# Moving the first B tiles of a fused matmul and RMS norm to the software DMA queue, and splitting A's first load over both hardware queues

## The chip, the cores and the metric

The kernel runs on one core of a Trainium2 chip. The metric is the device time of one execution in microseconds. TensorE is called PE below, VectorE DVE, ScalarE ACT, GpSimd POOL and SyncE SP. DMAs that SP and ACT issue run on the hardware queues, those of GpSimd on the software queue.

## The reference

```python
m, k, n = 2048, 2048, 2048            # a, b, gamma float32
x = np.matmul(a, b)
rms = np.sqrt(np.mean(x ** 2, axis=-1, keepdims=True) + eps)
return (gamma * x / rms).astype(np.float32)
```

## The kernel before

The first four blocks of 128 rows ("the head") are computed while A and B still arrive. The contraction goes by eight pairs of 128: a pair takes 512 rows by 256 columns of A (0.5 MB in fp32) and 256 rows of B's left half (1 MB in fp32, cast to bf16). A is transposed on PE. The first pair comes over the hardware queues in fp32 and is cast on the core; all later pairs come over the software queue, which casts in flight.

```python
    # first pair: hardware queues, fp32
    nc.sync.dma_start(out=a0f, in_=a[0:HB * P, 0:W2].rearrange("(r p) k -> p r k", p=P))
    for t in range(2):
        nc.scalar.dma_start(out=b0f[t], in_=b[t * P:(t + 1) * P, 0:HALF])
    ...
    def load_b(j, kp):                       # software queue, fp32 -> bf16
        nc.gpsimd.dma_start(
            out=raw[j][kp],
            in_=b[kp * W2:(kp + 1) * W2, j * HALF:(j + 1) * HALF].rearrange(
                "(t p) n -> p t n", p=P))

    def load_head(kp):                       # A block, then B tile, of one pair
        nc.gpsimd.dma_start(
            out=ah(kp),
            in_=a[0:HB * P, kp * W2:(kp + 1) * W2].rearrange("(r p) k -> p r k", p=P))
        load_b(0, kp)
    ...
    load_head(1)
    identity_f = t_left[:, 2, KP - 1, 0:2 * P].bitcast(FP32)
    make_identity(nc, identity_f)
    for kp in range(2, 4):
        load_head(kp)
    ...                                      # 11 warm-up matmuls on PE
    def transpose_first():
        ...                                  # 8 fp32 transposes into view[0], view[1]
        for t in range(2):
            cast_first = [lambda: nc.vector.tensor_copy(out=raw[0][0][:, t, :CH],
                                                        in_=b0f[t][:, :CH]),
                          lambda: nc.scalar.copy(out=raw[0][0][:, t, CH:], in_=b0f[t][:, CH:])]
            move = [lambda h=h: nc.vector.tensor_copy(
                out=head_at[:, t, 2 * h:2 * h + 2, :], in_=view[t][:, 2 * h:2 * h + 2, :])
                for h in range(2)]
            for work in (cast_first + move if t == 0 else move + cast_first):
                work()
    ...
    for kp in range(KP):                     # the head, left half
        if kp + 4 < KP:
            load_head(kp + 4)
        ...                                  # 14 matmuls, transposes of the next pair, 2 matmuls
```

In what follows, pairs are counted from one: "the second pair's B tile" is `raw[0][1]`, "the fifth" is `raw[0][4]`.

Of the kernel before, what the change touches and what calls it, by code (L numbers as in the profile page):

```python
# [8 lines left out]
FP32 = mybir.dt.float32  # L9
# [8 lines left out]
def kernel(  # L18
# [13 lines left out]
    nc = tc.nc  # L32
    P = 128
# [4 lines left out]
    W2 = 2 * P  # L38
    MB = M // P
    CH = 512  # L40
    NCH = N // CH
    HALF = N // 2
    HB = 4
# [15 lines left out]
    early = consts.tile([P, 6 * 2048], BF16, name="early")  # L59
    head_at = consts.tile([P, KT, HB, P], BF16, name="head_at")  # L60
    raw = [[consts.tile([P, 2, HALF], BF16, name=f"b_{j}_{kp}") for kp in range(KP)]
           for j in range(2)]
# [2 lines left out]
    sums = [t_left, t_right]  # L65

    a0f = early[:, 0:2048].bitcast(FP32).rearrange("p (r k) -> p r k", r=HB)
    b0f = [early[:, 2048 + t * 2048:2048 + (t + 1) * 2048].bitcast(FP32) for t in range(2)]
    NAH = 6
    ah_slot = [early[:, 6144 + s * 1024:6144 + (s + 1) * 1024].rearrange("p (r k) -> p r k", r=HB)  # L70
               for s in range(NAH)]
# [16 lines left out]
        return (at_even, at_odd)[(mb // 2) % 2][:, mb % 2]  # L88


    nc.sync.dma_start(out=a0f, in_=a[0:HB * P, 0:W2].rearrange("(r p) k -> p r k", p=P))
    for t in range(2):
        nc.scalar.dma_start(out=b0f[t], in_=b[t * P:(t + 1) * P, 0:HALF])

    def ah(kp):
        return ah_slot[(kp - 1) % NAH]

    def load_b(j, kp):
# [5 lines that stand above are left out]
    def load_head(kp):  # L104
# [4 lines that stand above are left out]
# [15 lines left out]
    def wait_for(src):  # L124

        nc.gpsimd.tensor_copy(out=pace, in_=src)

    load_head(1)
    identity_f = t_left[:, 2, KP - 1, 0:2 * P].bitcast(FP32)
    make_identity(nc, identity_f)  # L130
# [19 lines left out]
    def transpose_first():  # L150
        bank = [ps_t.tile([P, CH], FP32, name="tbank"), ps_a.tile([P, CH], FP32, name="acc")]
        view = [b.rearrange("p (r m) -> p r m", r=HB) for b in bank]
        for t in range(2):
            for r in range(HB):
                nc.tensor.matmul(view[t][:, r, :], a0f[:, r, t * P:(t + 1) * P], identity_f,
                                 is_transpose=True, start=(r == 0), stop=(r == HB - 1))
        for t in range(2):
            cast_first = [lambda: nc.vector.tensor_copy(out=raw[0][0][:, t, :CH],
                                                        in_=b0f[t][:, :CH]),
                          lambda: nc.scalar.copy(out=raw[0][0][:, t, CH:], in_=b0f[t][:, CH:])]  # L160
            move = [lambda h=h: nc.vector.tensor_copy(
                out=head_at[:, t, 2 * h:2 * h + 2, :], in_=view[t][:, 2 * h:2 * h + 2, :])
                for h in range(2)]
            for work in (cast_first + move if t == 0 else move + cast_first):
                work()

    def transpose_head(kp):
        bank = ps_t.tile([P, CH], FP32, name="tbank")
# [263 lines left out]
    for r in range(HB):  # L432
        x_tile(r, 0)
    early_sums = {4: ((2,), 0, 6), 5: ((5,), 0, 7), 6: ((1,), 0, KP)}
    transpose_first()
    for kp in range(KP):
        if kp + 4 < KP:
# [393 lines left out]
```

## Time and profile before

| | before |
|---|---|
| median of 3 runs | 222.53 us (222.32 to 222.62) |
| span of the profiled execution (a run of 222.97 us) | 221.2 us |
| PE busy | 95% of the span |
| A's first load landed, last engine | 6.26 us |
| B's first two tiles landed, last engine | 5.13 and 8.68 us |
| second pair's B tile landed, last engine | 12.26 us |
| fifth pair's B tile landed, last engine | 25.05 us |

The landings are read from the semaphore increments in the trace. A DMA here is complete when all sixteen engines have added theirs, so a tile is there when its slowest engine is.

First the chain of waits that ended last, in order of time: start, length, what. DMA pieces run from issue to landing.

```profile
5.65 0.70 POOL b L99
...
6.70 0.65 POOL early L105
7.35 17.70 DMA b<-in_b_dram
25.05 0.04 issue
25.10 1.67 PE acc L384 x7
26.77 0.45 PE tbank L172 x8
27.21 1.51 PE acc L384 x7
28.73 0.43 PE tbank L415 x2
29.16 1.51 PE acc L384 x7
...
68.17 139.98 PE acc L289 x648
```

From the fifth pair's B tile on, PE never waits until 208.2 us; before it the chain is that tile's DMA. A pair costs PE 1.51+0.45+1.51+0.43 = 3.9 us, and the software queue delivers one every 3.83 us (16.08 less 12.26, the last engine's landings of the second and the third pair's B tiles). The two are so close that PE cannot catch up: a tile that comes late anywhere in the head is paid in full.

The timeline of the first microseconds (start, busy time, engine, line, operation, and in brackets the idle time before it and who ended it):

```profile
0.74 0.46 SPq L91 DMA_DIRECT2D early<-in_a_dram  x1
0.74 0.90 ACTq L93 DMA_DIRECT2D early<-in_b_dram  x2
...
1.25 0.94 POOL L105 DMA_DIRECT2D early<-in_a_dram  x1 [0.80 <-POOLq L812]
...
7.54 2.88 PE L384 MATMUL acc<-b,head_at 128*128 128x512 bf16 x12
...
8.70 0.62 ACT L160 CAST b<-early 128x512 bf16<-128x512 f32 x1 [2.93 <-DMA early<-in_b_dram]
...
12.30 1.67 PE L384 MATMUL acc<-b,head_at 128*128 128x512 bf16 x7
...
25.10 1.67 PE L384 MATMUL acc<-b,head_at 128*128 128x512 bf16 x7 [0.85 <-DMA b<-in_b_dram]
```

PE's second pair starts at 12.30, as soon as its B tile is there (12.26), and before the fifth pair PE waits 0.85 us. Last, the table of windows: stretch, its length, busy time of PE, PEld (PE's weight loads), DVE, ACT and POOL with their counts, granted clock, mean DMA share, GB/s. The GB/s count bytes as written, so a load that casts reads twice as much.

```profile
4.00:6.00 2.00, 1.87 (x6) 0.55 (x4) 0.74 (x1) 0.62 (x1) 2.00 (x4) 1.00 1.06 350
6.00:8.00 2.00, 1.52 (x11) 1.08 (x12) 0.94 (x3) 0.00 (x0) 2.00 (x11) 1.00 0.80 214
8.00:10.00 2.00, 2.00 (x10) 0.86 (x9) 0.91 (x3) 0.62 (x1) 0.10 (x1) 1.00 1.31 207
```

The last line is the software stream: 207 GB/s written, 414 read. Up to 8 us almost all traffic is the hardware queues' (the DMA records show the first software packet at 6.27 us).

### The profile page before, as it was taken

How to read it: one execution, taken by the hardware profiler on the slowest of the kernel's cores; microseconds unless marked ns; L12 is line 12 of the kernel's file. 1: busy time of each engine (PE TensorE's matmuls, PEld its weight loads, DVE VectorE, ACT ScalarE, POOL GpSimd, SP SyncE). 2: the span in 40 equal slices, each digit the busy share in tenths (PEclk: the TensorE clock that was granted, in tenths of full speed). 3: DMA queues.
4: the chain of work that ended last, by engine and by line, in shares of the span. 5: the costliest groups of instructions: out<-in, count | busy, mean ns of one | idle time of the engine just before them, and what ended most of it. 6: DMA issues, size and time to landing. Idle time of an engine off the chain costs nothing.

```text
span 221.2 us, 3022 instructions
## 1 busy us (share of the span) xinstructions
PE 210.0 (95%) x1035; PEld 97.7 (44%) x1035; DVE 167.4 (76%) x330; ACT 128.1 (58%) x263; POOL 29.4 (13%) x59
## 2 busy tenths in 40 slices
PE   7899899999999999999999999999999999999950
PEld 2445454444455444444444444444444444444430
DVE  2428789999988898969696639855794759797691
ACT  3110001830698898678945997389738995334570
POOL 7634323220000001200110002000200000000040
PEclk9999999999999999999999999999999999999996
DMA  6999999999938596956799249955798349044045
GB/s 184 223 202 209 203 208 210 211 211 238 426 114 357 187 291 120 316 230 150 219 308 397 79 88 266 367 221 95 187 302 367 69 90 381 32 190 193 1 190 191
DMA packets 36321, 47.13 MB, mean 213 GB/s; under 512 B 21969, under 2 KB 26065, under 8 KB 34897
## 3 DMA queue, kind: packets, MB, share of 16 engines
q0 software_dynamic: 9936, 23.33, 41.7%
q1 hardware_dynamic: 25936, 22.29, 33.6%
q10 hardware_dynamic: 432, 1.31, 2.0%
q8 instruction: 8, 0.13, 0.2%
q14 instruction: 9, 0.07, 0.1%
HBM read 34.60 MB, written 16.78 MB: 232 GB/s over the span
## 4 chain that ended last, share of the span: by engine, by line
PE 83%; DMA 8%; POOL 3%; DVE 2%; issue 1%; ACT 1%; DVEq 0%; ACTq 0%; POOLq 0%
PE acc L289 69%; PE acc L384 12%; DMA b<-in_b_dram 8%; POOL early L105 1%; POOL b L99 1%; DVE x L709 1%; PE tbank L415 1%; PE tbank L172 1%; DVE x L712 1%; ACT sq L307 0%; PE tbank L189 0%; PE acc L189 0%; DVE a L709 0%; ACT sq L778 0%; DVE x L786 0%
## 5 line engine op out<-in xcount | busy, mean ns | idle before, releaser
L289 PE MATMUL acc<-b,s 128*128 128x512 bf16 x408 | 92.1, 379 | 0.0
L289 PEld LDWEIGHTS <-s 128*128 128x128 f16 (+1 forms) x512 | 49.9, 98 | 59.9 <-DVE s L264 0.4
L384 PE MATMUL acc<-b,head_at 128*128 128x512 bf16 x176 | 41.9, 379 | 1.0 <-DMA b<-in_b_dram 0.9
L307 ACT ACTIVATE sq<-x 128x512 bf16<-128x512 f32 x54 | 34.0, 630 | 6.9 <-DVE x L709 3.0
L366 DVE SCALAR_TENSOR_TENSOR x<-x,r,gamma_sb 128x1024 f32<-128x1024 f32 x28 | 34.8, 1281 | 0.7
L223 ACT ACTIVATE sq<-a 128x1024 bf16<-128x1024 f32 x24 | 25.3, 1054 | 2.4 <-DMA a<-in_a_dram 1.9
L384 PEld LDWEIGHTS <-head_at 128*128 128x128 bf16 x176 | 16.8, 98 | 20.6 <-issue 1.9
L246 ACT ACTIVATE head_at<-a,s 128x2048 f16<-128x2048 f32 x10 | 20.0, 1998 | 3.7 <-DVE s L233 3.7
L426 ACT COPY x<-acc 128x512 f32<-128x512 f32 x6 | 3.4, 586 | 25.7 <-PE acc L384 25.7
L289 PEld LDWEIGHTS <-head_at 128*128 128x128 f16 (+1 forms) x112 | 10.9, 98 | 13.2
L289 PE MATMUL acc<-early,head_at 128*128 128x512 bf16 x64 | 14.5, 379 | 0.0
L289 PEld LDWEIGHTS <-at_even 128*128 128x128 f16 x96 | 9.4, 98 | 11.3
L289 PE MATMUL acc<-early,s 128*128 128x512 bf16 x56 | 14.4, 379 | 0.0
L264 DVE TENSOR_TENSOR s<-head_at 128x1024 f16<-128x1024 f16 (+5 forms) x22 | 13.4, 635 | 0.1
L596 DVE TENSOR_TENSOR x<-x,x 128x512 f32<-128x512 f32 x9 | 6.2, 692 | 8.8 <-ACT x L594 8.3
L99 POOL DMA_DIRECT2D b<-in_b_dram x15 | 10.6, 706 | 16.0 <-DMA b<-in_b_dram 13.4
L578 ACT COPY x<-acc 128x512 f32<-128x512 f32 x9 | 5.2, 574 | 11.6 <-PE acc L289 11.5
L289 PE MATMUL acc<-t_left,s 128*128 128x512 bf16 x48 | 11.3, 379 | 0.0
L280 DVE TENSOR_TENSOR b<-b 128x1024 bf16<-128x1024 bf16 x16 | 10.8, 684 | 0.2
L289 PE MATMUL acc<-t_left,head_at 128*128 128x512 bf16 x48 | 10.9, 379 | 0.0
L289 PE MATMUL acc<-t_left,at_even 128*128 128x512 bf16 x48 | 10.8, 379 | 0.0
L289 PE MATMUL acc<-early,at_even 128*128 128x512 bf16 x48 | 10.8, 379 | 0.0
(111 smaller groups left out, 216.7 us busy)
## 6 DMA issues: line engine op xcount, KB each, us to landing
out_dram<-x SPq DMA_DIRECT2D x30, 512.0 KB, 3.8
a<-in_a_dram POOLq DMA_DIRECT2D x10, 1024.0 KB, 8.7
b<-in_b_dram POOLq DMA_DIRECT2D x15, 512.0 KB, 17.5
a<-in_a_dram POOLq DMA_DIRECT2D x4, 512.0 KB, 16.6
early<-in_a_dram POOLq DMA_DIRECT2D x7, 256.0 KB, 14.8
early<-in_b_dram ACTq DMA_DIRECT2D x2, 512.0 KB, 5.9
gamma_sb<-in_gamma_dram POOLq DMA_DIRECT2D x1, 1024.0 KB, 14.8
early<-in_a_dram SPq DMA_DIRECT2D x1, 512.0 KB, 5.5
```

The costliest lines, as they stand in the source:

```text
L99: nc.gpsimd.dma_start(out=raw[j][kp], in_=b[kp * W2:(kp + 1) * W2, j * HALF:(j + 1) * HALF].rearrange("(t p) n -> p t n", p=P))
L223: nc.scalar.activation(out=junk, in_=a32[mb][:, h * HALF:(h + 1) * HALF], func=ACTF.Square, scale=2.0 ** -8, accum_out=n2[:, h:h + 1])
L246: nc.scalar.activation(out=a16[mb], in_=a32.pop(mb), func=ACTF.Copy, scale=factor.pop(mb))
L264: nc.vector.tensor_tensor(out=sum_of(g, s)[:, lo:hi, :], in0=x[:, lo:hi, :], in1=y[:, lo:hi, :], op=op)
L280: nc.vector.tensor_tensor(out=flat[:, 1:3, :], in0=flat[:, 1:3, :], in1=flat[:, 0::3, :], op=ALU.add)
L289: nc.tensor.matmul(bank, lhsT[:, kp, :], rhs, start=(start and kp == 0), stop=(kp == KP - 1), skip_group_check=not start)
L307: nc.scalar.activation(out=sq[:, 0:CH], in_=src, func=ACTF.Square, scale=inv_sqrt_n, accum_out=msq[mb][:, c:c + 1])
L366: nc.vector.scalar_tensor_tensor(out=x, in0=x, scalar=inverse_of[mb], in1=gamma_sb[:, h * HALF:(h + 1) * HALF], op0=ALU.mult, op1=ALU.mult)
L384: nc.tensor.matmul(bank, head_at[:, kt, r, :], head_rhs(c, kt), start=(kt == 0), stop=(kt == KT - 1))
L426: copy(out=x_chunk(*g), in_=banks[g])
L578: nc.scalar.copy(out=c, in_=one[1])
L596: nc.vector.tensor_tensor(out=t, in0=t, in1=x12, op=ALU.add)
```

## The change

The intent: the stream of the software queue is the bottleneck of the head, and it seems to start late because 1.5 MB in fp32 go before it on slower hardware queues. So only A's 0.5 MB stay there, by halves on both queues; B's first tiles join the faster software stream, which casts them, and four casts on the core disappear. The copies of the transposes are shared by DVE and ACT.

```diff
-    nc.sync.dma_start(out=a0f, in_=a[0:HB * P, 0:W2].rearrange("(r p) k -> p r k", p=P))
-    for t in range(2):
-        nc.scalar.dma_start(out=b0f[t], in_=b[t * P:(t + 1) * P, 0:HALF])
+    for h, queue in enumerate((nc.sync, nc.scalar)):
+        queue.dma_start(out=a0f[:, 2 * h:2 * h + 2, :],
+                        in_=a[2 * h * P:(2 * h + 2) * P, 0:W2].rearrange("(r p) k -> p r k", p=P))
...
+    for t in range(2):
+        nc.gpsimd.dma_start(out=raw[0][0][:, t, :], in_=b[t * P:(t + 1) * P, 0:HALF])
     load_head(1)
...
-        for t in range(2):
-            cast_first = ...          # DVE and ACT cast B's tile t
-            move = ...                # DVE copies the transposes
-            for work in (cast_first + move if t == 0 else move + cast_first):
-                work()
+        for t, copy in enumerate((nc.vector.tensor_copy, nc.scalar.copy)):
+            for h in range(2):
+                copy(out=head_at[:, t, 2 * h:2 * h + 2, :], in_=view[t][:, 2 * h:2 * h + 2, :])
```

More of the change, by code (lines that the diff above doesn't have):

```diff
@@ L67 @@
     a0f = early[:, 0:2048].bitcast(FP32).rearrange("p (r k) -> p r k", r=HB)
-    b0f = [early[:, 2048 + t * 2048:2048 + (t + 1) * 2048].bitcast(FP32) for t in range(2)]
     NAH = 6
@@ L156, in transpose_first @@
                                  is_transpose=True, start=(r == 0), stop=(r == HB - 1))
-        for t in range(2):
-            cast_first = [lambda: nc.vector.tensor_copy(out=raw[0][0][:, t, :CH],
-                                                        in_=b0f[t][:, :CH]),
-                          lambda: nc.scalar.copy(out=raw[0][0][:, t, CH:], in_=b0f[t][:, CH:])]
-            move = [lambda h=h: nc.vector.tensor_copy(
-                out=head_at[:, t, 2 * h:2 * h + 2, :], in_=view[t][:, 2 * h:2 * h + 2, :])
-                for h in range(2)]
-            for work in (cast_first + move if t == 0 else move + cast_first):
-                work()
+        for t, copy in enumerate((nc.vector.tensor_copy, nc.scalar.copy)):
+            for h in range(2):
+                copy(out=head_at[:, t, 2 * h:2 * h + 2, :], in_=view[t][:, 2 * h:2 * h + 2, :])
     def transpose_head(kp):
```

## The prediction

> **What bounds the kernel now.** From 25.1 us to 208.2 us TensorE is the whole chain of waits, with no idle stretch. Before that the chain is one piece: 17.7 us of "DMA b<-in_b_dram" (7.35 to 25.05 us), the fifth B tile of the software queue. The timeline shows TensorE paced by B earlier too: the tiles of pairs 1 and 3 land at 12.26 and 20.14 us, their matmuls start at 12.30 and 20.18. A pair costs TensorE 3.9 us (1.51+0.45+1.51+0.43 in the chain) and the software queue 3.83 us (landing to landing). So everything after 25.05 us moves with the landing of the fifth B tile, and that moves with the moment the software stream starts at full rate.
>
> **What the first loads do now.** By the DMA records the hardware queues carry A's 0.5 MB and B's 1 MB from about 1.6 to 8.5 us, at about 230 GB/s. The software queue, issued at 1.25 us, has its first packet at 6.3 us, few until 8 us, and then reads about 420 GB/s (a 1 MB B tile, cast, per 2.48 us; a 0.5 MB A block per 1.3 us). Its first A block lands at 9.72 us, so it starts, in effect, at 8.45.
>
> **What changes.** The hardware queues keep only 0.5 MB. B's 1 MB goes ahead of the software stream, with the cast. Removed: four casts (0.62, 0.62, 0.74, 0.43 us) on VectorE and ScalarE. Two transposed halves (0.37 us each) move to ScalarE. GpSimd gets two more issues (0.5 to 0.7 us each) before the identity; the warm-up matmuls run to 5.9 us, so this has slack. The Trainium skill (DMA: Bandwidth & Descriptors, SWDGE vs HWDGE vs iDMA) says that a cast in flight needs the software path; the same page gives that path about 1 us to the first byte. The trace agrees where the queues are quiet: 1.25 us at 64.3 us.
>
> **Sum (estimate).** A's two halves land near 4.5 us. B needs 1 MB at 420 GB/s, 2.5 us, mostly behind them: first tile near 5.7, second near 7. The stream then starts in effect near 7.0 instead of 8.45: 1.4 us earlier: pair 1's B tile near 10.8, the fifth tile near 23.6. TensorE starts on the first pair near 7.1 (7.54 now), reaches pair 1 near 11.0 (12.30 now) and follows. I discount 0.2 us for a late software start. All of it is on the critical path.
>
> Predicted: 221.3 us, range 220.2 to 222.7. Faster by over 2%: 0.01; within 2%: 0.98; slower: 0.01.
>
> **What would show it.** Software queue's first packets at 2.5 to 4.5 us; A landing before 5.5; first pair's matmuls running without the gap around 9 us; pair 1's B tile landing near 10.8; the DMA piece of the chain ending near 23.6; the rest of the chain 183 us as now.
>
> **What would make it wrong.** (1) The 6.3 us is the software path's own cold start, not hardware traffic ahead of it: then B's second tile lands at 8.8 us and the stream starts 0.3 us later than now; gain zero or a small loss. (2) The fifth tile is late partly because one of the 16 engines lags: its last landings come 1.5 us after the others, following a 16 KB instruction fetch at 20 to 22 us. If that lag falls elsewhere, up to about 1 us more is won; or lost. (3) ScalarE's copies hold the first matmuls.

## The result

The changed kernel took 222.84 us (median of 4 runs, 222.49 to 223.03), the kernel before 222.57 us beside it: a ratio of 1.0012, 95% interval 0.9998 to 1.0027. Ratios are computed as the mean time of one kernel's runs over that of the other's of the same rounds, so they are not quite the ratio of the medians quoted. The predicted 1.2 us did not come, and the time lies just above the predicted range (220.2 to 222.7). Measured again on another chip it was 222.47 us beside 222.76, ratio 0.9992 (0.9974 to 1.0010).

| last engine's landing, us | before | before again | changed | changed again | predicted |
|---|---|---|---|---|---|
| A's first load | 6.26 | 6.37 | 4.27 | 4.23 | 4.5 |
| B's first two tiles | 5.13, 8.68 | 5.21, 8.76 | 6.92, 8.76 | 6.23, 8.68 | 5.7, 7 |
| second pair's B tile | 12.26 | 12.34 | 12.59 | 12.53 | 10.8 |
| the same, mean of 16 engines | 11.98 | 11.94 | 11.84 | 11.74 | |
| fifth pair's B tile | 25.05 | 24.63 | 24.54 | 24.48 | 23.6 |
| span of the profiled run | 221.2 | 221.1 | 220.7 | 220.7 | |

The spans look 0.4 us better, but the four profiled runs are not like the timed ones: the two of the kernel before took 222.97 and 222.87 us, slower than most of its runs, and those of the changed kernel 222.49 and 222.44, at its fast end. The timed runs decide: no gain.

The chain of waits of the changed kernel:

```profile
1.23 0.71 POOL b L128
1.95 6.81 DMA b<-in_b_dram
8.76 0.29 issue
9.05 15.50 DMA b<-in_b_dram
24.59 1.67 PE acc L379 x7
26.26 0.45 PE tbank L167 x8
26.70 1.51 PE acc L379 x7
28.21 0.43 PE tbank L410 x2
28.65 1.51 PE acc L379 x7
```

It now starts with B's first load itself, which takes 6.8 us from issue to landing. The chain still names the fifth pair's tile, but PE was all but ready for it: it waited 0.10 us there (0.85 in the kernel before). Its timeline, for the same places:

```profile
0.74 0.45 SPq L91 DMA_DIRECT2D early<-in_a_dram  x1
...
1.23 1.25 POOL L128 DMA_DIRECT2D b<-in_b_dram  x2 [0.79 <-POOLq L807]
...
7.42 2.76 PE L379 MATMUL acc<-b,head_at 128*128 128x512 bf16 x12
...
10.16 0.62 PE L167 MATMUL tbank<-identity,early 128*128 128x128 bf16 x8
...
12.63 1.46 PE L379 MATMUL acc<-b,head_at 128*128 128x512 bf16 x6 [0.47 <-DMA b<-in_b_dram]
...
24.59 1.67 PE L379 MATMUL acc<-b,head_at 128*128 128x512 bf16 x7
```

PE starts the first pair 0.12 us earlier, ACT's copies hold nothing up, the casts are gone, and then PE waits 0.47 us for the second pair's B tile, which comes later than before. From there on PE's own work sets the time, but for the 0.10 us at the fifth pair (the timeline prints idle times from 0.15 us on). The windows show why the tile is late:

```profile
4.00:6.00 2.00, 2.00 (x6) 0.83 (x5) 0.36 (x2) 0.00 (x0) 1.93 (x5) 1.00 1.13 134
6.00:8.00 2.00, 1.92 (x12) 1.28 (x11) 0.76 (x2) 0.62 (x2) 2.00 (x11) 1.00 1.01 120
8.00:10.00 2.00, 2.00 (x11) 0.78 (x8) 0.00 (x0) 0.02 (x1) 1.16 (x2) 1.00 1.30 206
```

The software stream is running from 4 us on, but writes 134 and 120 GB/s instead of 206. The packets' time falls far less than the bytes (share 1.13 and 1.01 against 1.30; packets overlap, so it can exceed 1): each packet takes longer. By the DMA records B's 4 KB reads took 276 ns each from 4 to 8 us, and 173 ns from 9 us on. The kernel before shows the same on the hardware queue: B's 4 KB packets took 225 ns from 5 to 8 us, where they had taken 160 from 3.5 to 5 us. So B's first megabyte was there no sooner by the one route than by the other: at 8.68 to 8.76 us in all four profiles.

The second thing is the spread. These are the sixteen engines' completions of the second pair's B tile, from the trace:

```
before   11.76 11.78 11.80 11.88 11.89 11.90 11.91 11.94 12.00 12.01 12.02 12.07 12.12 12.18 12.24 12.26
changed  11.23 11.27 11.40 11.41 11.45 11.81 11.82 11.85 11.91 11.92 12.03 12.07 12.09 12.19 12.31 12.59
```

The average engine is 0.15 us earlier, the last one 0.33 later. Once the packets run at their steady 173 ns, what an engine has lost is not made up: one and two pairs later (15.07 to 16.47 for the third pair's tile, 18.88 to 20.25 for the fourth's) the spread is still 1.4 us. (The landings do not name their engine; that it is the same ones is read from the pattern, which repeats from tile to tile.)

### The profile page after: what moved, and what is told of

Same layout as the page of the kernel before. It is cut to its first block, busy times and chain, and to the rows that moved or that the text cites. A ratio compares the mean times of both kernels' runs of the same rounds, so it can differ in the third digit from the quotient of the medians.

```text
span 220.7 us, 3001 instructions
## 1 busy us (share of the span) xinstructions
PE 209.3 (95%) x1015; PEld 98.0 (44%) x1035; DVE 165.3 (75%) x326; ACT 127.4 (58%) x263; POOL 30.4 (14%) x61
## 4 chain that ended last, share of the span: by engine, by line
PE 83%; DMA 10%; DVE 2%; issue 1%; ACT 1%; POOL 0%; DVEq 0%; ACTq 0%; POOLq 0%
PE acc L284 69%; PE acc L379 12%; DMA b<-in_b_dram 10%; DVE x L704 1%; PE tbank L410 1%; PE tbank L167 1%; DVE x L707 1%; ACT sq L302 0%; PE tbank L184 0%; PE acc L184 0%; POOL b L128 0%; DVE a L704 0%; ACT sq L773 0%; DVE x L781 0%; DVE x L785 0%
## 5 line engine op out<-in xcount | busy, mean ns | idle before, releaser
L379 PE MATMUL acc<-b,head_at 128*128 128x512 bf16 x171 | 41.2, 379 | 0.9 <-DMA b<-in_b_dram 0.5
L275 DVE TENSOR_TENSOR b<-b 128x1024 bf16<-128x1024 bf16 x16 | 10.8, 684 | 0.2
L284 PE MATMUL acc<-early,at_even 128*128 128x512 bf16 x48 | 10.8, 379 | 0.1
L284 PE MATMUL acc<-t_left,head_at 128*128 128x512 bf16 x48 | 10.8, 379 | 0.0
L284 PE MATMUL acc<-t_left,at_even 128*128 128x512 bf16 x47 | 10.8, 379 | 0.1
```

What stands on the lines that cost most here:

```text
L275: nc.vector.tensor_tensor(out=flat[:, 1:3, :], in0=flat[:, 1:3, :], in1=flat[:, 0::3, :], op=ALU.add)
L284: nc.tensor.matmul(bank, lhsT[:, kp, :], rhs, start=(start and kp == 0), stop=(kp == KP - 1), skip_group_check=not start)
L379: nc.tensor.matmul(bank, head_at[:, kt, r, :], head_rhs(c, kt), start=(kt == 0), stop=(kt == KT - 1))
```

## The experiments

All are edits of the changed kernel unless said otherwise. "Last" is the last engine's landing.

### What makes the first reads slow

**One issue instead of two.** Theories named there: FORM, TIME, PLACE.

```diff
-    for t in range(2):
-        nc.gpsimd.dma_start(out=raw[0][0][:, t, :], in_=b[t * P:(t + 1) * P, 0:HALF])
+    load_b(0, 0)
     load_head(1)
```

> The changed kernel with B's first two tiles in one software issue, the form of all later B tiles. Theory FORM (two [128 x 1] issues send the 16 engines to rows in an order that reads slowly): B's 4 KB packets take their later 173 ns throughout, the pair has landed by about 6.5 us and the time falls by about 1.5 us, to 221.3. Theory TIME (whatever is read in large packets between about 4.5 and 7.7 us is slow): the packets still average over 250 ns there, B lands at 8.5 to 9 us and the time stays at 222.6 to 223.0. Theory PLACE (rows 0 to 255 of B are slow to read): as TIME.

B landed at 8.87, the second pair's tile at 12.69. Time 224.83 us (222.94 to 225.5), ratio 1.0081. The profile is of its fastest run; in it PE waited 2.75 us for the pair, since one issue has one landing. FORM falls.

**The second pair first.**

```diff
-    for t in range(2):
-        nc.gpsimd.dma_start(out=raw[0][0][:, t, :], in_=b[t * P:(t + 1) * P, 0:HALF])
     load_head(1)
+    for t in range(2):
+        nc.gpsimd.dma_start(out=raw[0][0][:, t, :], in_=b[t * P:(t + 1) * P, 0:HALF])
```

> The second pair's loads are issued before the first pair's B tiles. TIME: the second pair's B tile, now read from about 5 us on, has packets averaging over 250 ns until about 7.7 us, and B's first tiles, read after that, have 173 ns. FORM or PLACE: the second pair's B tile reads at 173 ns at once, and the first pair's tiles are slow (over 250 ns) wherever they come, at 7 to 12 us. The time is expected longer by 1 to 3 us under all, as TensorE starts later.

The second pair's B tile was now the slow one: its packets averaged 311 to 313 ns from 7 to 8.5 us, and it landed between 8.89 and 11.51 us. From 9.5 us on, when the first pair's tiles were read after it, packets took 185 ns, falling to 174 by 11 us. So it is not the rows 0 to 255 and not the form. Time 229.24 us, because PE starts late.

**Other rows** (wrong result).

```diff
-        nc.gpsimd.dma_start(out=raw[0][0][:, t, :], in_=b[t * P:(t + 1) * P, 0:HALF])
+        nc.gpsimd.dma_start(out=raw[0][0][:, t, :], in_=b[(10 + t) * P:(11 + t) * P, 0:HALF])
```

> Wrong result on purpose: the first pair's B tiles are read from rows 1280 to 1535 instead of 0 to 255, in the same two issues. PLACE: their packets take 173 ns, they land by about 6.5 us, the time falls by about 1.5 us. FORM or TIME: they average over 250 ns between 4.5 and 7.7 us and land at 8.5 to 9 us, time unchanged.

They landed at 7.77 and 9.16 us, with one engine 1.4 us behind the others; and then the second pair's tile was slow as well (last 14.10, packets of 262 to 308 ns from 10 to 11 us). PLACE falls. TIME is damaged too, since 10 to 11 us lies outside its window. Time 225.47 us.

**B alone** (the rest is issued when both tiles have landed).

```diff
-    load_head(1)
     identity_f = t_left[:, 2, KP - 1, 0:2 * P].bitcast(FP32)
     make_identity(nc, identity_f)
+    hold = consts.tile([P, 1], FP32, name="hold")
+    for t in range(2):
+        nc.gpsimd.tensor_copy(out=hold, in_=raw[0][0][:, t, 0:1])
+    load_head(1)
```

> GpSimd waits until both of the first pair's B tiles have landed before it issues any other load. Theory CROWD (descriptor writing or the queued loads of the next pairs slow the first B tiles): they now read at 173 ns and land by about 6.8 us. TIME, FORM, PLACE: they are as slow as before and land at 8.5 to 9 us. In either case the stream behind them starts about 2 us late and the time grows by 1 to 3 us.

B landed at 6.12 and 7.37 us, 1.4 us earlier than with the queue filled behind it: CROWD has some part in it. But the slow stretch came back in the second pair's B tile, and that settles TIME:

```profile
4.00:6.00 2.00, 2.00 (x11) 1.12 (x10) 0.00 (x0) 0.00 (x0) 0.00 (x0) 1.00 1.07 151
...
10.00:12.00 2.00, 0.13 (x2) 0.13 (x3) 0.00 (x0) 0.00 (x0) 2.00 (x4) 0.95 1.32 194
12.00:15.00 3.00, 2.70 (x12) 1.25 (x11) 0.69 (x1) 0.27 (x1) 2.88 (x12) 0.50 0.99 123
```

From 12 to 15 us, where the changed kernel writes 210 GB/s, this one writes 123. Time 226.2 us, in which there is also TensorE's granted clock of 0.50 in that stretch.

**Held behind the first tile only.** As above, with one wait, for tile 0.

```diff
+    nc.gpsimd.tensor_copy(out=hold, in_=raw[0][0][:, 0, 0:1])
     load_head(1)
```

> The changed kernel, but GpSimd waits until B's first tile has landed before it issues the second pair and all later loads. CROWD (queued and just written loads slow the first B reads): B lands at 6.1 and 7.4 us as in the run that waited for both, the second pair's issue at 6.3 joins without a pause, its B tile lands by about 11.2, time about 221.3 to 221.8. If the stall comes back in the second pair's B tile, as it did there at 12 to 15 us, that tile lands at 12.5 to 14.5 and the time is 222.8 to 224.5.

B landed at 5.89 and 7.95, the second pair's tile between 12.99 and 15.76. PE's timeline:

```profile
15.81 2.72 PE L381 MATMUL acc<-b,head_at 128*128 128x512 bf16 x6 [3.48 <-DMA b<-in_b_dram]
```

Time 225.49 us (224.81 to 226.78), ratio 1.0130. Making room for B's first tiles speeds these up and slows the next.

**Smaller reads**, 1 KB for the first pair's B; then 2 KB for all eight left B tiles.

```diff
 # e5 (and make_identity goes before load_head(1))
+    for c in range(4):
+        nc.gpsimd.dma_start(out=raw[0][0][:, :, c * W2:(c + 1) * W2],
+                            in_=b[0:W2, c * W2:(c + 1) * W2].rearrange("(t p) n -> p t n", p=P))
 # e6, in load_b, for j == 0, and load_b(0, 0) for the first pair
+        for c in range(2):
+            nc.gpsimd.dma_start(out=raw[j][kp][:, :, c * CH:(c + 1) * CH], in_=...)
```

> The changed kernel with B's first two tiles in four software issues of 256 columns, so in 1 KB reads like A's (the identity is made before the second pair's issues). Theory FIRST LARGE READS (the first 4 KB reads of a stream stall, whatever they are; A's 1 KB reads never showed it): the first pair's B reads at 59 to 65 ns a packet and lands by about 6.5 us, but the second pair's B tile, now the first in 4 KB reads, averages over 230 ns a packet and lands at 12 us or later; time 222 to 224 us. Theory FIRST BYTES OF B (whatever of B comes first stalls): the 512 B packets average over 80 ns, B lands after 8 us, the second pair's tile is fast. If neither holds, all is fast and the time is about 221.

> The changed kernel with all eight left B tiles loaded in two column halves each, 2 KB reads. If the stall needs 4 KB reads, no packet stalls and the first pair's B lands by about 6.8 us, time about 221 us. If it is the start of a read stream whatever the packet (down to 2 KB), B still lands at 8 to 9 us and the time is 222.5 to 225.

With 1 KB reads B's last part landed at 9.10 us, its packets averaging 60 to 81 ns against 59 later: slowed a little, but four issues of 0.7 us each take their time as well. One engine fell behind by 1.0 to 1.1 us in the last two parts (7.37 to 8.41 us, 8.00 to 9.10), and the second pair's tile landed between 11.75 and 15.23. Neither theory fits cleanly. Time 225.41 us (223.38 to 226.53). With 2 KB reads B landed at 10.42, three engines 1 us or more behind the others; 224.75 us (224.08 to 226.04). The stall does not need 4 KB reads.

**One row, and contiguous rows** (both wrong).

```diff
 # e10
+        nc.gpsimd.dma_start(out=raw[0][0][:, t, :], in_=b[t, 0:HALF].partition_broadcast(P))
 # e11
+        nc.gpsimd.dma_start(out=raw[0][0][:, t, :],
+                            in_=b[t * 64:(t + 1) * 64, :].rearrange("q (c n) -> (q c) n", c=2))
```

> Wrong result on purpose: the changed kernel with the first pair's B tiles filled by reading one 4 KB row of B 128 times per tile, same issues, sizes and destinations. SOURCE (the stall is in reading many rows of memory at once): their packets take about 173 ns and they land by 7 us; the second pair's tile, then the first of many rows, stalls instead. OTHER SIDE (the stall lies in the engines, the descriptors or the writing): packets average over 230 ns between 4.5 and 7.5 us and land at 8.3 to 9.2 us, as in the changed kernel.

> Wrong result on purpose: the first pair's B tiles are read as contiguous 512 KB (64 whole rows each) instead of 128 half rows 8 KB apart. PITCH (the 8 KB pitch puts all engines on the same part of the memory): packets at about 173 ns, landed by 7 us. Otherwise as the changed kernel, 8.3 to 9.2 us.

With one row the packets were fast (189 ns on average from 4 to 8 us), but there were fewer of them, with gaps between, and B still landed at 8.82. That is neither of the two answers foreseen: the limit is not the time of a packet as such. With contiguous rows most engines were done by 6.74 us (the last at 8.16), and the slow stretch moved to the second pair's tile, whose packets took 254 ns from 9 to 11 us against 173 in the changed kernel. That tile landed at 12.42, as ever. Times 223.08 and 222.98 us.

### What it is worth, and where the bill goes

**Half of B's first tiles, and none** (both wrong; the rest is set to a constant).

```diff
 # e8
-        nc.gpsimd.dma_start(out=raw[0][0][:, t, :], in_=b[t * P:(t + 1) * P, 0:HALF])
+        nc.gpsimd.dma_start(out=raw[0][0][:, t, 0:CH], in_=b[t * P:(t + 1) * P, 0:CH])
+    nc.vector.memset(raw[0][0][:, :, CH:], 0.5)
 # e7
-    for t in range(2):
-        nc.gpsimd.dma_start(out=raw[0][0][:, t, :], in_=b[t * P:(t + 1) * P, 0:HALF])
+    nc.vector.memset(raw[0][0], 0.5)
```

> Wrong result on purpose: only columns 0 to 511 of the first pair's B tiles are loaded (0.5 MB, two issues, 2 KB reads). If the stall is per byte of B at the start (about 200 GB/s), they land by 6.2 to 6.7 us, the second pair's tile by 10.5 to 11, time 221.0 to 221.8. If it is a fixed bill of some 20 engine-us that goes over to whatever large reads follow, the second pair's tile stalls too and lands at 11.3 to 12.5, time 221.8 to 223.

> Wrong result on purpose: the changed kernel without the first pair's B loads (the two tiles are set to a constant). If the arrival of the software stream at the head is what the time waits for, it falls until TensorE's own work binds: first pair from about 7.1 us, second from about 11.0, the fifth from about 22.7, then the same 181.4 us from the last partial product on, so a span near 219 us, a time of 220.5 to 221.0. If something else holds the head (the right half of B, the copies), the time stays above 222. The stall of the first large reads is expected to appear in the second pair's B tile, as in the run that issued it first.

This is the clearest pair. With half of B (landed at 6.08 and 6.97) the second pair's tile landed at 11.58, the fifth at 23.34, and PE had no wait for a load left from the second pair on: 221.65 us, span 219.9. With no first B load at all, 1 MB less than the changed kernel, the tile landed at 11.81: taking out 2.5 us of stream at full rate won 0.7 to 0.8 us.

```profile
4.00:6.00 2.00, 2.00 (x13) 1.34 (x12) 0.12 (x1) 0.00 (x0) 2.00 (x4) 1.00 1.30 155
6.00:8.00 2.00, 1.92 (x11) 0.84 (x10) 0.64 (x2) 0.65 (x2) 2.00 (x11) 1.00 0.92 99
8.00:10.00 2.00, 2.00 (x16) 1.03 (x14) 0.39 (x1) 0.00 (x0) 0.86 (x2) 1.00 1.00 111
10.00:12.00 2.00, 0.74 (x4) 0.29 (x3) 0.30 (x1) 0.58 (x1) 0.00 (x0) 1.00 1.20 179
```

The slow stretch lasts until after 10 us, on the second and third pairs. Its engines ended 3.3 us apart (8.48 to 11.81). Time 222.14 us instead of the 220.5 to 221.0 expected. Whatever is taken out ahead of it, the second pair's tile came no earlier than 11.5 us in any run.

### The two halves of the change

**Only A by halves, B behind it on both hardware queues** (an edit of the kernel before).

```diff
-    nc.sync.dma_start(out=a0f, ...)
-    for t in range(2):
-        nc.scalar.dma_start(out=b0f[t], in_=b[t * P:(t + 1) * P, 0:HALF])
+    for h, queue in enumerate((nc.sync, nc.scalar)):
+        queue.dma_start(out=a0f[:, 2 * h:2 * h + 2, :], ...)
+    for t, queue in enumerate((nc.sync, nc.scalar)):
+        queue.dma_start(out=b0f[t], in_=b[t * P:(t + 1) * P, 0:HALF])
```

> The kernel before with only A's load split over both hardware queues, B's fp32 tiles behind it, one on each queue, casts as before. Theory SAME BILL (1 MB of B costs about 5 us at the start of the run by either route): A lands near 4.2 us instead of 6.3, B's second tile at 8 to 9 us, the software stream's first A block at 9.5 to 10.2, time 222.3 to 223.0. A rival, that the software route is what is slow: B lands by 7.5 us and the time is about 221.5.

**Only B by the software queue**, A whole on SP.

```diff
-    for h, queue in enumerate((nc.sync, nc.scalar)):
-        queue.dma_start(out=a0f[:, 2 * h:2 * h + 2, :], ...)
+    nc.sync.dma_start(out=a0f, in_=a[0:HB * P, 0:W2].rearrange("(r p) k -> p r k", p=P))
```

> The changed kernel with A's first load whole on one hardware queue, as before the change. A lands near 5.0 us instead of 4.2, in place of which nothing else moves: B's tiles at 8.5 to 9.2 us, time 222.6 to 223.5, within 0.3 us of the changed kernel. If the split of A matters for the start of the software stream, it is 0.5 to 1 us slower.

With B on the hardware queues its packets ran from 3.45 us and it landed at 8.46, as SAME BILL said: 5.0 us for the megabyte, against 5.3 by the software queue (3.44 to 8.76). PE waited 1.48 us in the first pair for VectorE, whose copies there stand behind its cast of B's first tile (landed at 7.71), and for no load after it. The software stream's first A block landed at 9.60 and the second pair's tile at 12.04: 222.83 us, ratio 1.0016. With A whole on one queue it landed at 4.12 us, no later than by halves (4.27 and 4.23). The Trainium skill (DMA: Bandwidth & Descriptors, Issuing engines are not separate DMA queues) says that the queues share the same sixteen DMA engines and that issuing from several saves only the sequencer's issue time; this agrees. Still that kernel was slower, 224.00 us (223.73 to 224.40), ratio 1.0066: its B tiles landed at 8.68 and 10.26 and the second pair's tile at 14.08, engines 2.2 us apart. I had expected no difference. Its profile has 28 to 50 KB written by the software queue in each half microsecond from 4 to 5 us, against 60 to 88 KB in the changed kernel; why is open.

### Second profiles

These two are the changed kernel and the kernel before, with no edit.

> The changed kernel once more, for a second profile beside these. Median 222.6 to 223.1; B's first tiles at 6.5 to 7.5 and 8.4 to 9.2 us; the second pair's B tile lands with 1 to 2 us between its first and its last engine (0.5 us in the kernel before).

> The kernel before once more, for a second profile: its first profile was of an execution of 222.97 us, slower than its timed ones. Time within 0.2 us of the kernel before. If the late landing of the fifth B tile (25.05 us, 1.3 us behind the other engines) is usual, it is late by 1 us or more again and the profiled span is near 221.2; if it was a bad draw, the tile lands near 24.5 and the span is near 220.7, as in both profiles of the changed kernel.

Both are in the table above: 222.47 and 222.65 us. The fifth tile was late again in the kernel before, 0.87 us behind its other engines (1.32 in the first profile).

### A version meant to beat both

A's 1 KB reads beside the slow B packets kept their 59 ns in the kernel before. So the second pair's A block was put on the hardware queues too, in fp32 behind the first's halves, and cast half by ACT and half by DVE; in a further kernel also the third pair's.

```diff
+    for kp in afast:                       # {1}, or {1, 2}; fp32 views of free space in "early"
+        for h, queue in enumerate((nc.sync, nc.scalar)):
+            queue.dma_start(out=afast[kp][:, 2 * h:2 * h + 2, :],
+                            in_=a[2 * h * P:(2 * h + 2) * P, kp * W2:(kp + 1) * W2].rearrange(
+                                "(r p) k -> p r k", p=P))
...
+        if kp not in afast:
             nc.gpsimd.dma_start(out=ah(kp), ...)
...
+        for kp in afast:                   # after the copies of the first transposes
+            nc.scalar.copy(out=ah(kp)[:, 0:2, :], in_=afast[kp][:, 0:2, :])
+            nc.vector.tensor_copy(out=ah(kp)[:, 2:4, :], in_=afast[kp][:, 2:4, :])
```

> A version meant to beat both: the changed kernel with the second pair's A block also in fp32 on the hardware queues (1 KB reads, behind the first's halves), cast half by ScalarE and half by VectorE, so that the software stream carries B's first two tiles and the second pair's B tile back to back. If the first B reads stall and A's 1 KB reads can fill their gaps, the second pair's B tile lands 1 us earlier than 12.55, at 11.2 to 11.7, the fifth at 23.2 to 23.7, and TensorE's own work binds: time 221.3 to 221.9. If the bill only moves (the tile lands at 12.0 to 12.7 whatever is taken away ahead of it), time 222.3 to 223.0.

> The same with the second and the third pair's A blocks on the hardware queues. The software stream is then 0.5 MB shorter again before the third pair's B tile. If the gaps are filled: the second pair's B tile at 11.4 to 12.0 (more hardware traffic beside B's first tiles), the third's at 14 to 14.6, TensorE binds, time 221.2 to 221.9. If the bill only moves, 222.3 to 223.5.

With one block the second pair's B tile landed at 11.76, between 11.34 and 11.76 over the engines, and the time was 221.99 us, ratio to the kernel before 0.9974 (0.9957 to 0.9991). It was not timed beside the changed kernel, whose medians were 222.84 and 222.47 us. Part of it is not as argued: A's block was there by 5.72 us, so it went ahead of B rather than into its gaps, and B's tiles came at 6.95 and 9.27. What the trace shows in its place is that B's three tiles run back to back with the engines close together; that the gain comes from this is my reading. B's packets took 172 to 183 ns until 6 us and 267 to 285 from 6 to 8.5 us: it is not the very first reads that are slow. PE's timeline:

```profile
9.31 1.24 PE L390 MATMUL acc<-b,head_at 128*128 128x512 bf16 x5 [0.65 <-DMA b<-in_b_dram]
...
12.21 1.46 PE L390 MATMUL acc<-b,head_at 128*128 128x512 bf16 x6
...
24.33 1.67 PE L390 MATMUL acc<-b,head_at 128*128 128x512 bf16 x7 [0.26 <-DMA b<-in_b_dram]
```

PE waits for B's second tile in the first pair, then runs through to the fifth pair, whose last engine is late. With two blocks the third pair's A ran beside B's first tiles, all were slower (10.64, second pair's tile 13.31), and the time was 222.96 us, ratio 1.0023.

> The version with the second pair's A block on the hardware queues once more, in five rounds. It is expected 0.2 to 0.4% faster than the kernel before (221.8 to 222.2 us) with the interval below 1; the second pair's B tile at 11.5 to 12.0 us with under 0.7 us between its first and last engine; the fifth tile's last engine again about 1 us behind the rest, after TensorE's instruction fetch.

In five more rounds beside the kernel before: 221.99 us (221.83 to 222.46), ratio 0.9981 (0.9968 to 0.9995), the tile between 11.33 and 11.65, the fifth tile's last engine 0.73 us behind the rest. It is a small gain, about 0.2%, but it held.

## Why the prediction was right or wrong

- *What bounds the kernel.* Right. In most traces the span is 181.4 us more than the start of the last partial product of the head's left half (181.15 to 181.77 in all); what arrives late there is paid one for one, and leaving out half of B's first tiles took 0.8 us off (one look at 221.65 us, against 222.47 for the changed kernel in its second measurement).
- *The software queue starts late because hardware traffic is ahead of it, not from a cold start.* Supported, not proved. Its first packet came at 3.44 us with 0.5 MB ahead, at 4.84 and 4.97 with 1 MB, at 6.27 with 1.5 MB; but at 4.89 in the run with 1.5 MB of A, where the third block was still on its way. So cold start, risk (1), is not what happened. That risk (1) named B's second tile at 8.8 us and a gain of zero, which is what was measured, is luck: the first packets came within the 2.5 to 4.5 us predicted, and the loss came after them.
- *A lands near 4.5 us.* Right (4.27).
- *"B needs 1 MB at 420 GB/s, 2.5 us, mostly behind them: first tile near 5.7, second near 7."* This is the step that failed. 420 GB/s is the rate of the stream once it flows; the first reads of B do not get it. B took from 3.44 to 8.76 us, 5.3 us or about 200 GB/s, and 5.0 us on the hardware queues behind the same A (the run with A by halves only). Slower packets are one part (276 ns against 173); with one row B's packets took 189 ns, yet it landed at 8.82, so they are not the whole. The trace of before already held the warning: the hardware packets of B took 225 ns from 5 to 8 us where they had taken 160 just before. I had put that down to the hardware route.
- *"The stream then starts in effect near 7.0": second pair's tile near 10.8.* It was 12.59, against 12.26 before: a loss of 0.33 us in place of a gain of 1.46, together 1.79. On the average engine the tile was 0.15 earlier, so 1.31 of it are the slow start; the last engine was 0.75 behind the average instead of 0.27, which is the other 0.48. The prediction had not thought of the spread at all.
- *The fifth tile near 23.6.* It came at 24.54 and 24.48; the kernel before had 25.05 and 24.63. Some of the loss is given back there, since one engine's lag counted for less: in the kernel before it stood out 1.32 and 0.87 us behind the next one, in the changed kernel 0.42 and 0.51, and PE waited 0.85 and 0.44 us there against 0.10 and 0.09. That was named as risk (2). The traces tie the lag to the 16 KB instruction fetch at 21.5 us, whose one packet takes 0.94 to 0.98 us in these four: with the second pair first the fetch came at 28.30 us instead, the fifth tile's last engine was 0.07 us behind the next, and only in the tiles after 28.3 us had one engine moved from 0.11 to 1.24 us behind the first. But no run took the fetch away.
- *The removed casts, the moved copies, the extra issues.* Off the critical path, as said; risk (3) did not come. PE started the first pair 0.12 us earlier instead of 0.4.
- *The rest of the chain, 183 us.* Right: 24.59 to 207.64 us.
- *The range.* "Within 2%" was right. The upper end, 0.2 us above the old time, left no room for the case that the slow start of reads goes along with B.

What stays open is the mechanism of the slow first reads. The runs show that it is not the rows, not the form of the issue, not a fixed stretch of time, not the queue and not only the size of the reads; that it is eased when nothing is queued behind; and that easing it for one tile moves it to the next. Contiguous rows landed sooner, one row did not. No theory named above fits every run.

One rival was not tested. At the start GpSimd issues its loads back to back, 0.5 to 0.8 us each, and most of the slow stretches lie where it does so: 4.48 to 8.46 us in the changed kernel, slow from 4.5 to 8; 7.96 to 14.88 us in "B alone", slow from 11.5 to 15. No run spaced these issues. It cannot be all: "B alone" had packets of 294 and 269 ns from 4 to 5 us, when no issue had run since 2.48 us, and "Other rows" had 223 to 308 ns from 9 to 12 us, with single issues as in the steady stream, in which packets take 173.

## What to carry to other kernels

A rate read from the steady part of a stream is not the rate of its first megabyte; cost the start of a stream with the packets that the profile shows at a start, whatever queue they are on. A load that all DMA engines share is there when the slowest has landed its part, so look at the first and last engine as well as the mean: a spread that arose at the start here stayed in the steady stream. When a cost is about equal by two routes, suspect that it belongs to neither route, and take it away altogether in one run before building on either.

## What the Trainium skill lacked or had wrong

- DMA: Bandwidth & Descriptors (Bandwidth) gives rates by transfer size, but nothing on the rate in a stream's first microseconds: here the cast stream wrote 120 to 134 GB/s from 4 to 8 us and 206 after it, and the slow stretch moved (123 GB/s from 12 to 15 us when the second pair's loads were held back).
- The same page has the row pitch as a cause of slow copies between HBM tensors (Latency and other measured facts), with 207 GB/s at a pitch of 512 KiB, near the 214 that it calls full. B's pitch is 8 KB and its first reads were slow; reading contiguous rows made the first pair faster (6.2 and 8.2 us), yet the next tile was slow instead. The entry does not explain this.
- That engines which fall behind in a stream stay behind has no page that I found: in the changed kernel the second, third and fourth pair's tiles had 1.36, 1.40 and 1.37 us between the first and last engine.
- Runtime: NRT & Kernel Launch (Instruction fetch mechanics) calls the cost of a 16 KiB instruction block mostly hidden. The trace has such a fetch on the DMA engines at 21.5 us, and one engine's next B tile 0.87 to 1.32 us behind the others in the kernel before, on the critical path; in another run the fetch came at 28.3 us and the lag after it, but no run was without a fetch.
- DMA: Bandwidth & Descriptors gives the software path about 1 us to its first byte. With hardware traffic ahead it was 2.2 us (0.5 MB) and 5.0 us (1.5 MB) after the issue, and 1.25 us where the queues were quiet.
